# Places of the first small products behind the large ones, in a hybrid recurrent decoder step

## The chip, the cores and the metric

One core of a Trainium2 chip runs the whole step. The metric is the time of one execution on the device in microseconds, as a median over runs. TensorE (PE in the rows) multiplies, VectorE (DVE), ScalarE (ACT) and GpSimd (POOL) do the rest, SyncE (SP) issues the DMAs.

## What is computed

Two layers act on 1024 prompt tokens and 8 single tokens of width 1024. Cut to what matters here, a layer is:

```
h = rmsnorm(x, norm_g)
p = h @ w_in                       # split into q, f, i, z, ... of three groups
o_a = head_rmsnorm(gated_recurrence(q_a, k_a, i_a, log_f)) * silu(z_a)    # 6 heads, 64 x 64
o_b = head_rmsnorm(gated_recurrence(q_b, k_b, v_b, log_g)) * silu(z_b)    # 6 heads, 32 x 64
o_c = s5 group with its own gate
x + concat(o_a, o_b, o_c) @ w_out
```

The recurrence runs by chunks: within a chunk `att = k^T q` under a causal mask times v, and between chunks the carried state S times q. `head_rmsnorm` needs the mean square over each head's 64 rows, which is a product with a block of ones. The 8 single tokens each take one step of the same recurrences from given states.

## The kernel before, in words

**Large products.** A tile of 128 output columns of `w_in` or `w_out` is one `gemm_tile` (L302): three blocks of tokens (384, 384, 264), in each block 8 steps k, in each step three matmuls (high and low parts of weights and input). So a tile has 72 large products, written `ps_g` in the rows; only tile 0 of layer 0 writes to other banks, so that up to any time of layer 0 there have been 72 more than the rows of `ps_g` count. A layer has 25 tiles from `w_in`, in the order UC 2, VB 3, QB, KB, QK, VA 3, then F and Q in turn three times, ZB 3, ZC 2, ZA 3, and then 8 from `w_out`. Weights come by DMA and are split into `wh` (ACT) and `wl` (POOL and DVE in turn).

**Small work by threads.** Everything else is in Python generators. `tick()` lets each living thread go on to its next `yield`; `gemm_tile` ticks after the fourth step k of each block and after each block, thus after every 12 large products. The place of a small product in the program is so the number of large ones that stand before it. There are threads for the S5 group (`s5_thread`, then `glu`), for turning values (`turn`, transposes of `vf`), for the single tokens (`decode`, L918), for the two parts of the B group (`unit_b`, two and one pairs of heads; L1116) and the three pairs of A heads (`unit_a`, L968). A lock lets one of b0, b1, a0, a1, a2 into its products at a time. A tensor of one row per channel and one column per token takes one of 16 slots; `room(n)` (L106) ticks without any large product until n are free.

**A unit's steps.** `unit_a`: transposes of k, `kv()` (state updates, then scaled by DVE L1045 and scanned, L897), `att()`, two yields, `inter()` (state times q, rows `ps_o<-qs,Sp`), the masks of `att` (DVE, L1077), a yield, `intra()` (`ps_o<-atts,v`), then for each of two halves `headnorm` (L900) and a yield. `headnorm` squares and splits on ACT and DVE (`sl` L907), yields, multiplies with the ones (`ps_aux<-sl,obd`), then takes the root. `unit_b` has four (b0) or two (b1) rounds of a yield, `outputs` (L1184, rows `ps_o<-qb,Sp`), the next round's `att` and mask (L1181), and a `headnorm`. `decode` ends with one small product per token (`ps_aux<-dS,qbd`), a copy, a transpose (`ident,dV`), a copy and 4 or 8 small DMAs.

**The order of the work.** The launch says `schedule_with_timeline_sim=True`. A planner writes out each engine's order when the program is built, by a model of time of its own: among the instructions of an engine that it holds ready, the one that the program issued first goes next. On the chip each engine then keeps to that order. A dependency of class `NoSync` is an order for the planner alone; it makes no semaphore.

PSUM has three `g` banks for the large products, two `o` banks and three `aux` banks for the small ones.

Of the kernel before, what the change touches and what calls it, by code (L numbers as in the profile page):

```python
# [14 lines left out]
P = 128  # L15
# [23 lines left out]
def tile_hybrid_step(ctx: ExitStack, tc: tile.TileContext, a: dict, nl=NL, limit=RANGE):  # L39
# [42 lines left out]
    def psum(tag, shape=(P, 512), dt=F32):  # L82
        n = {"g": 3, "o": 2, "aux": 3}[tag]
        return ps.tile(list(shape), dt, tag=tag, bufs=n, name=nm("ps_" + tag))
# [60 lines left out]
    def act(out, in_, func, **kw):  # L145
        return S.activation(out=out, in_=in_, func=func, **kw)  # L146
# [8 lines left out]
    def mm(out, lhsT, rhs, start=True, stop=True):  # L155
        return TE.matmul(out=out, lhsT=lhsT, rhs=rhs, start=start, stop=stop)  # L156

    def behind(i, others):

        for x in others:  # L160
            tc.add_manual_dep(getattr(i, "ins", i), getattr(x, "ins", x).name,
                              mybir.DependencyInfo(mybir.DependencyClass.Sync, mybir.DependencyReason.DATA), reason="bank")


    ident = cst.tile([P, P], F32, name="ident")
    maskA = cst.tile([P, 64], I8, name="maskA")
# [135 lines left out]
    def gemm_tile(i, blocks, rhs, evac, last=True, ks=range(KD), banks="ggg"):  # L302

        for b in blocks:
            o, n = BLK[b]
            p = psum(banks[b]) if isinstance(banks[b], str) else banks[b]
            for j, k in enumerate(ks):
                wh, wl = W.get(i, k)
                rh, rl = rhs(k, b)
                mm(p[:, :n], wh, rh, start=(j == 0), stop=False)  # L310
                mm(p[:, :n], wh, rl, start=False, stop=False)
                mm(p[:, :n], wl, rh, start=False, stop=(j == KD - 1))
                if j == 3:
                    tick()
                if b == blocks[-1] and last:
                    W.do_split(4 * (i + 1) + min(3, (j + 1) // 2))
            evac(b, p[:, :n])
            if b == blocks[0]:
                W.do_split(4 * (i + 1) + 1)
            tick()  # L320
# [339 lines left out]
    def layer(l, slow=False):  # L660
# [239 lines left out]
        def headnorm(po, dst, n=512):  # L900

            sq = tmp("sq", [P, 512])
            sh = tmp("sh", [P, 512], F32R)
            sl = tmp("sl", [P, 512], F32R)
            act(out=sq, in_=po, func=AF.Square)
            act(out=sh, in_=sq, func=AF.Copy)
            V.tensor_tensor(out=sl, in0=sq, in1=sh.bitcast(F32), op=ALU.subtract)  # L907
            yield
            pn = psum("aux")
            mm(pn, obd, sl, start=True, stop=False)  # L910
            mm(pn, obd, sh, start=False, stop=True)
            rs = tmp("sq", [P, 512])
            act(out=rs, in_=pn, func=AF.Ln, scale=1.0 / 64.0, bias=epsc)
            act(out=rs, in_=rs, func=AF.Exp, scale=-0.5)
            run = lambda x: x.rearrange("p (c t) -> p c t", t=n)
            V.tensor_tensor(out=dst if n < 512 else run(dst), in0=run(po), in1=run(rs), op=ALU.mult)

        def decode(pr, nh, kd, f8, k8, q8, head0, u0, sin, sout):  # L918

            yield from dec_lock.take()  # L920
            qbd = tmp("qbd", [P, 8, 32])[:pr]
            G.memset(qbd, 0.0)
            for h in range(nh):
                V.tensor_copy(out=qbd[h * kd:(h + 1) * kd, :, h], in_=q8[h * kd:(h + 1) * kd, :])
            sbs = []
            for b0 in (0, 4):
                sb = tmp("dS", [P, 4, 64], bufs=2)[:pr]
                vb = tmp("dV", [P, 4, 64])[:pr]
                SY.dma_start(out=sb, in_=sin[:, b0:b0 + 4, :])
                for h in range(nh):  # L930
                    SY.dma_start(out=vb[h * kd:(h + 1) * kd], in_=vdd[b0:b0 + 4, (head0 + h) * 64:(head0 + h) * 64 + 64]
                                 .unsqueeze(0).to_broadcast([kd, 4, 64]))
                yield
                G.tensor_tensor(out=sb, in0=sb, in1=f8[:, b0:b0 + 4].unsqueeze(2).to_broadcast([pr, 4, 64]), op=ALU.mult)
                G.tensor_tensor(out=vb, in0=vb, in1=k8[:, b0:b0 + 4].unsqueeze(2).to_broadcast([pr, 4, 64]), op=ALU.mult)
                G.tensor_tensor(out=sb, in0=sb, in1=vb, op=ALU.add)
                yield
                SY.dma_start(out=sout[:, b0:b0 + 4, :], in_=sb)
                sbs.append(sb)
            yield  # L940

            po = psum("aux")
            for i, sb in enumerate(sbs):
                for b in range(4):
                    mm(po[32 * b:32 * b + 32, 64 * i:64 * i + 64], qbd[:, 4 * i + b, :], sb[:, b, :])
            stg = tmp("dV", [P, 4, 64]).rearrange("p a b -> p (a b)")[:, :P]
            act(out=stg, in_=po[:, :P], func=AF.Copy)
            po = psum("aux")
            TE.transpose(out=po[:, :P], in_=stg, identity=ident)
            stg = tmp("dO", [P, 4, 4])[:, :nh]  # L950
            act(out=stg, in_=po[:, :P].rearrange("p (b h) -> p h b", h=32)[:, :nh], func=AF.Copy)
            for h in range(nh):
                u, hf = divmod(h, 2)
                for i in range(2):
                    SY.dma_start(out=odec[64 * hf:64 * hf + 64, u0 + u, 4 * i:4 * i + 4], in_=stg[64 * i:64 * i + 64, h, :])
            dec_lock.give()
            decodes[0] += 1
# [10 lines left out]
        def unit_a(j, s1, s2, qs):  # L968
# [67 lines left out]
            def kv():  # L1036
                p = [psum("aux").rearrange("p (c v) -> p c v", v=64) for _ in range(2)]
                for c in range(16):
                    pr_, par = divmod(c, 2)
                    for h in range(2):  # L1040
                        mm(p[par][64 * h:64 * h + 64, pr_, :], ktm[64 * par:64 * par + 64, pr_, 64 * h:64 * h + 64],
                           vA[64 * par:64 * par + 64, pr_, (2 * j + h) * 64:(2 * j + h) * 64 + 64])
                x = on[:, :T].rearrange("p (v k r) -> p r k v", k=8, r=2)
                for par in range(2):
                    V.tensor_tensor(out=x[:, par], in0=p[par], in1=ac.rearrange("p (k r) -> p r k", r=2)[:, par]  # L1045
                                    .unsqueeze(2).to_broadcast([P, 8, 64]), op=ALU.mult)
                states(Sp, on, 16)
# [4 lines left out]
            def att():  # L1052
                p = [psum("aux") for _ in range(2)]
                for pair in range(8):
                    for par in range(2):
                        t0 = (2 * pair + par) * 64
                        for h in range(2):
                            mm(p[h][64 * par:64 * par + 64, pair * 64:pair * 64 + 64], kt[64 * h:64 * h + 64, t0:t0 + 64],
                               qt[64 * h:64 * h + 64, t0:t0 + 64])
                return p  # L1060

            def inter(po):

                for pair in range(8):
                    for par in range(2):
                        c = 2 * pair + par
                        for h in range(2):
                            ph = slice(64 * h, 64 * h + 64)
                            if c:
                                x = mm(po[par][ph, pair * 64:pair * 64 + 64], S3[ph, c - 1, :], qt[ph, c * 64:c * 64 + 64],  # L1070
                                       start=(pair == 1 - par), stop=False)
                                if pair == 7:
                                    yield x

# [16 lines left out]
            if j == 0:  # L1091
                for x in atts:
                    G.memset(x, 0.0)
            kv()
            p = att()
            yield
            yield
# [18 lines left out]
        def unit_b(ti, s, q, k):  # L1116
# [67 lines left out]
            def outputs(hp, hf, po):  # L1184

                for cc in range(4):
                    c = 4 * hf + cc
                    for g in range(2):
                        hd = 2 * hp + g
                        if c:  # L1190
                            mm(po[64 * g:64 * g + 64, cc * P:cc * P + P], S3[32 * hd:32 * hd + 32, c - 1, :],
                               q[32 * hd:32 * hd + 32, c * P:c * P + P], start=(cc == 1 - hf), stop=False)
                for cc in range(4):
                    for g in range(2):
                        hd = 2 * hp + g
                        mm(po[64 * g:64 * g + 64, cc * P:cc * P + P],
                           vB[:, 4 * hf + cc, (h0 + hd) * 64:(h0 + hd) * 64 + 64], db[g][:, cc, :],
                           start=False, stop=(cc == 3))
# [433 lines left out]
```

## Time and profile before

| what | us |
|---|---|
| median of 3 runs (1051.87 to 1053.72) | 1052.39 |
| the profiled execution | 1056.13 |
| its span, first to last instruction | 1054.2 |
| PE busy in it | 994.6 |

The profile is of one execution, 3.7 us longer than the median. Times in the rows are microseconds from the span's start. PE matmuls overlap and their ends are modelled, so that PE's time is better read from starts and from waits; "idle before" is time in which an engine stood still, with what released it.

### The profile page before, as it was taken

The page shows a single profiled execution, that of the slowest core. Times are in us where ns is not written, and L with a number is a line of the kernel's source. Part 1 is how long each engine was busy: PE and PEld are TensorE (multiplying, and loading weights), DVE is VectorE, ACT ScalarE, POOL GpSimd, SP SyncE. Part 2 cuts the span into 40 slices and gives each one's busy share as a digit, 9 for nine tenths or more (in the row PEclk, how much of TensorE's full clock was granted, in tenths as well). Part 3 has the DMA queues.
Part 4 walks back from the last instruction along what each step waited for, and adds up shares of the span by engine and source line. Part 5 has one row for each costly group of instructions (what it writes and reads, how often), then busy time and mean ns, then how long its engine had stood idle before and what let it go on. Part 6 is the DMA issues. An engine that isn't in the chain of part 4 may idle for free.

```text
span 1054.2 us, 20947 instructions
## 1 busy us (share of the span) xinstructions
PE 994.6 (94%) x8071; PEld 940.2 (89%) x8071; DVE 649.4 (62%) x1333; ACT 479.2 (45%) x995; POOL 472.2 (45%) x668
## 2 busy tenths in 40 slices
PE   6899999999999899999999999999999989999992
PEld 5788898899988799999999999888998988999991
DVE  8986745744767746685464682684388775553344
ACT  7334224554434656633332423445554475664431
POOL 4685754115355535542181476431344453552233
PEclk9999999899999989999999999999999998999996
DMA  7131131111111121144323114112111112112313
GB/s 245 46 107 51 42 107 46 59 50 56 54 40 38 57 73 60 48 137 136 128 78 92 48 41 113 45 47 61 41 56 53 41 53 70 54 48 88 116 51 135
DMA packets 78811, 76.77 MB, mean 73 GB/s; under 512 B 24524, under 2 KB 60652, under 8 KB 78700
## 3 DMA queue, kind: packets, MB, share of 16 engines
q1 hardware_dynamic: 78700, 75.33, 23.6%
q8 instruction: 65, 1.06, 0.4%
q14 instruction: 46, 0.38, 0.1%
HBM read 58.01 MB, written 15.53 MB: 70 GB/s over the span
## 4 chain that ended last, share of the span: by engine, by line
PE 68%; DVE 15%; POOL 7%; ACT 3%; issue 3%; DMA 2%; SPq 1%; DVEq 0%; POOLq 0%; ACTq 0%
PE ps_g L156 54%; PE ps_aux L156 8%; PE ps_o L156 5%; DVE s5W L584 1%; DVE Sp L897 1%; ACT ep L146 1%; DVE ep L873 1%; PE ps_aux L850 1%; POOL wl L289 1%; DVE onorm L1045 1%; DMA x<-in_xT 1%; ACT sg L146 1%; DVE wl L289 1%; DVE sl L907 1%; POOL s5E L364 1%
## 5 line engine op out<-in xcount | busy, mean ns | idle before, releaser
L156 PE MATMUL ps_g<-hh,wl 128*128 128x384 f32 (+1 forms) x1176 | 382.1, 326 | 4.5 <-POOL wl L289 4.5
L156 PE MATMUL ps_g<-hh,wh 128*128 128x384 f32 (+1 forms) x1176 | 384.6, 327 | 0.0
L156 PE MATMUL ps_g<-lo,wh 128*128 128x384 f32 (+1 forms) x1176 | 380.9, 324 | 0.0
L156 PEld LDWEIGHTS ps_g<-hh,wl 128*128 128x128 f32 x1176 | 223.5, 190 | 8.8 <-POOL wl L289 6.8
L156 PEld LDWEIGHTS ps_g<-hh,wh 128*128 128x128 f32 x1176 | 223.7, 190 | 5.3 <-issue 3.1
L156 PEld LDWEIGHTS ps_g<-lo,wh 128*128 128x128 f32 x1176 | 223.8, 190 | 1.0
L289 POOL TENSOR_TENSOR wl<-raw,wh 128x256 fp32r<-128x256 f32 x127 | 109.6, 865 | 219.9 <-ACT wh L146 207.0
L146 ACT ACTIVATE wh<-raw 128x256 fp32r<-128x256 f32 x258 | 102.2, 411 | 123.9 <-PE ps_g L156 111.5
L156 PE MATMUL ps_g<-m,wh 128*128 128x384 f32 (+1 forms) x567 | 135.7, 321 | 0.0
L289 DVE TENSOR_TENSOR wl<-raw,wh 128x256 fp32r<-128x256 f32 x131 | 82.1, 627 | 42.3 <-ACT wh L146 34.5
L156 PEld LDWEIGHTS ps_g<-m,wh 128*128 128x128 f32 x567 | 98.9, 188 | 0.5
L156 PE MATMUL ps_g<-m,wl 128*128 128x384 f32 (+1 forms) x261 | 82.9, 320 | 0.0
L1350 POOL TENSOR_TENSOR z<-z,sg 128x384 f32<-128x384 f32 (+1 forms) x48 | 47.3, 986 | 44.8 <-ACT sg L146 43.6
L156 PEld LDWEIGHTS ps_g<-m,wl 128*128 128x128 f32 x261 | 49.0, 188 | 0.1
L741 DVE TENSOR_TENSOR z<-ps_g,rn 128x384 f32<-128x384 f32 (+1 forms) x48 | 24.4, 509 | 32.8 <-PE ps_g L156 32.7
L146 ACT ACTIVATE sg<-z 128x384 f32<-128x384 f32 (+1 forms) x48 | 23.4, 487 | 28.9 <-DVE z L1348 28.7
L1360 DVE SCALAR_TENSOR_TENSOR onorm<-z,vec,onorm 128x384 f32<-128x384 f32 (+1 forms) x36 | 23.0, 639 | 21.3 <-POOL z L1350 21.2
L156 PE MATMUL ps_g<-vx,wh 128*128 128x384 f32 (+1 forms) x129 | 34.1, 322 | 0.0
L146 ACT ACTIVATE sg<-sg,ones 128x384 f32<-128x384 f32 (+2 forms) x52 | 32.3, 622 | 0.8
L146 ACT ACTIVATE sg<-sg 128x384 f32<-128x384 f32 (+2 forms) x56 | 31.8, 568 | 1.7 <-DVE sg L778 0.8
L156 PE MATMUL ps_o<-qs,Sp 64*64 64x64 f32 x360 | 23.4, 301 | 8.6 <-DVE Sp L897 8.6
L156 PEld LDWEIGHTS ps_o<-qs,Sp 64*64 64x64 f32 x360 | 21.2, 199 | 10.8 <-DVE Sp L897 9.6
(385 smaller groups left out, 1802.1 us busy)
## 6 DMA issues: line engine op xcount, KB each, us to landing
raw<-in_wf SPq DMA_DIRECT2D x100, 256.0 KB
raw<-in_wo SPq DMA_DIRECT2D x32, 256.0 KB
x<-in_xT SPq DMA_DIRECT2D x16, 192.0 KB
ext<-in_xT SPq DMA_DIRECT2D x16, 192.0 KB
x1d<-ext SPq DMA_DIRECT2D x16, 192.0 KB
ext<-x1d SPq DMA_DIRECT2D x16, 192.0 KB
usd<-ucp SPq DMA_DIRECT2D x4, 512.0 KB
s5U<-usd SPq DMA_DIRECT2D x32, 64.0 KB
```

The source lines that it names most:

```text
L146: return S.activation(out=out, in_=in_, func=func, **kw)
L156: return TE.matmul(out=out, lhsT=lhsT, rhs=rhs, start=start, stop=stop)
L289: e.tensor_tensor(out=wl, in0=r, in1=wh.bitcast(F32), op=ALU.subtract)
L364: e.tensor_tensor(out=dr, in0=dr, in1=t, op=ALU.subtract)
L584: V.tensor_tensor_scan(out=W_[:, ri, q], data0=m8[:, q0 + q:q0 + q + 1].to_broadcast([P, P]), data1=W_[:, ri, q], initial=0.0, op0=ALU.mul ...
L741: V.tensor_tensor(out=dst[:, o:o + n], in0=p, in1=rn[:, o:o + n], op=ALU.mult)
L850: TE.transpose(out=p[:, c * P:(c + 1) * P], in_=f[:, t0:t0 + P], identity=ident)
L873: V.tensor_tensor_scan(out=g[:, cs], data0=zero[:pr].to_broadcast([pr, ch]) if plus is None else plus[:, cs], data1=x[:, cs], initial=0.0, ...
L897: V.tensor_tensor_scan(out=s[:, :64 * n], data0=s[:, :64 * n], data1=kv[:, :64 * n], initial=0.0, op0=ALU.mult, op1=ALU.add)
L907: V.tensor_tensor(out=sl, in0=sq, in1=sh.bitcast(F32), op=ALU.subtract)
L1350: G.tensor_tensor(out=z[:, c], in0=z[:, c], in1=sg[:, c], op=ALU.mult)
L1360: V.scalar_tensor_tensor(out=on[:, c], in0=z[:, c], scalar=g, in1=on[:, c], op0=ALU.mult, op1=ALU.mult)
```

## The change

`gemm_tile` remembers the third matmul of each step k, the last large product that the program has issued. `paced(i)` orders i behind that one (no semaphore). It is put on the first product of `headnorm`, of `att` and `inter` in `unit_a`, of `outputs` in `unit_b`, and on the first product and the transpose of `decode`: 34 instructions per layer. Yields are added: one in `headnorm`, one in `decode` before its transpose, two in `unit_a` between `kv()` and `att()`. Nothing is computed otherwise.

```diff
+    front = [None]
+    def paced(i):
+        if front[0] is not None:
+            tc.add_manual_dep(getattr(i, "ins", i), getattr(front[0], "ins", front[0]).name,
+                              mybir.DependencyInfo(mybir.DependencyClass.NoSync, mybir.DependencyReason.DATA), reason="pace")
+        return i
...
-                mm(p[:, :n], wl, rh, start=False, stop=(j == KD - 1))
+                front[0] = mm(p[:, :n], wl, rh, start=False, stop=(j == KD - 1))
...
             V.tensor_tensor(out=sl, in0=sq, in1=sh.bitcast(F32), op=ALU.subtract)
             yield
+            yield
             pn = psum("aux")
-            mm(pn, obd, sl, start=True, stop=False)
+            paced(mm(pn, obd, sl, start=True, stop=False))
...
-                    mm(po[32 * b:32 * b + 32, 64 * i:64 * i + 64], qbd[:, 4 * i + b, :], sb[:, b, :])
+                    x = mm(po[32 * b:32 * b + 32, 64 * i:64 * i + 64], qbd[:, 4 * i + b, :], sb[:, b, :])
+                    if i + b == 0:
+                        paced(x)
...
             act(out=stg, in_=po[:, :P], func=AF.Copy)
+            yield
             po = psum("aux")
-            TE.transpose(out=po[:, :P], in_=stg, identity=ident)
+            paced(TE.transpose(out=po[:, :P], in_=stg, identity=ident))
...
+                            if t0 + h == 0:
+                                paced(x)
...
+                                if c + h == 1:
+                                    paced(x)
...
             kv()
+            yield
+            yield
             p = att()
             yield
             yield
...
+                            if cc == 1 - hf and g == 0:
+                                paced(x)
```

The last three are in `att` and `inter` of `unit_a` and in `outputs` of `unit_b`, each on the first matmul.

## Rows read from the trace of the kernel before

**Rows 1.** The page: busy time, share of the span, instructions.

```profile
PE 994.6 (94%) x8071; PEld 940.2 (89%) x8071; DVE 649.4 (62%) x1333; ACT 479.2 (45%) x995; POOL 472.2 (45%) x668
```

**Rows 2.** Waits of PE over the span: in total, times, longest.

```profile
PE ps_o L156 <- DVE Sp L897: 8.6, 6, 2.3
...
PE ps_aux L156 <- DVE sl L907: 4.2, 4, 2.4
PE ps_aux L156 <- DVE onorm L1045: 3.8, 2, 2.1
PE ps_aux L850 <- DVE atts L1181: 3.1, 2, 1.9
...
PE ps_aux L949 <- ACT dV L146: 0.8, 1, 0.8
```

**Rows 3.** Stages: window, its length, busy time of each engine, PEclk, DMA share, GB/s.

```profile
144.00:246.00 102.00, 100.09 (x887) 88.91 (x886) 56.45 (x106) 47.13 (x86) 31.20 (x37) 0.97 0.20 56
...
275.00:382.00 107.00, 96.49 (x1225) 90.84 (x1224) 70.08 (x131) 49.77 (x103) 49.02 (x54) 0.92 0.16 48
...
652.00:755.00 103.00, 101.57 (x907) 90.90 (x906) 59.35 (x100) 49.03 (x87) 33.04 (x36) 1.00 0.19 55
...
784.00:898.00 114.00, 106.25 (x1291) 100.14 (x1290) 79.86 (x151) 62.28 (x127) 51.12 (x58) 0.94 0.19 57
```

**Rows 4.** Matmuls of ps_g alone, counted (x) up to the start of a small run.

```profile
0.00:279.19 279.19, 177.53 (x1007) 0.98 0.26 78
0.00:284.74 284.74, 179.21 (x1015) 0.98 0.26 78
0.00:304.10 304.10, 191.08 (x1087) 0.98 0.26 76
0.00:314.63 314.63, 200.92 (x1138) 0.97 0.25 76
0.00:367.42 367.42, 232.06 (x1321) 0.97 0.24 72
0.00:155.65 155.65, 98.50 (x540) 0.98 0.33 100
0.00:163.72 163.72, 101.65 (x557) 0.98 0.32 97
0.00:173.13 173.13, 106.40 (x586) 0.98 0.31 94
```

**Rows 5.** PE in order of time, layer 0, B units: start, us, what [idle before].

```profile
181.96 0.51 PE L156 MATMUL ps_o<-qb,Sp 32*64 32x128 f32 x4
184.38 0.66 PE L850 MATMUL ps_aux<-ident,vf 128*128 128x128 f32 x4 [1.91 <-DVE atts L1181]
...
190.55 0.67 PE L156 MATMUL ps_g<-hh,wh 128*128 128x384 f32 x1
```

**Rows 6.** DVE in order of time, the same stretch.

```profile
178.94 4.15 DVE L584 TENSOR_TENSOR_SCAN s5W<-sm,s5W 128x128 f32<-128x128 f32 x4
183.02 0.66 DVE L907 TENSOR_TENSOR sl<-sq,sh 128x512 fp32r<-128x512 f32 x1
...
184.22 0.71 DVE L1181 COPY_PREDICATED atts<-maskB,ps_aux 128x512 f32<-128x512 int8 x1
```

**Rows 7.** PE, the same run of products in layer 1.

```profile
690.72 0.66 PE L850 MATMUL ps_aux<-ident,vf 128*128 128x128 f32 x4 [1.21 <-DVE atts L1181]
...
694.56 0.42 PE L156 MATMUL ps_g<-hh,wh 128*128 128x384 f32 x1
```

**Rows 8.** PE, large products and a run of small ones beside each other.

```profile
212.86 0.42 PE L156 MATMUL ps_g<-lo,wh 128*128 128x384 f32 x1
213.11 0.33 PE L156 MATMUL ps_g<-hh,wl 128*128 128x384 f32 x1
213.38 0.99 PE L156 MATMUL ps_o<-qk,Sp 32*64 32x128 f32 x12
...
217.79 0.33 PE L156 MATMUL ps_g<-lo,wh 128*128 128x384 f32 x1
217.96 0.34 PE L156 MATMUL ps_g<-hh,wl 128*128 128x384 f32 x1
```

**Rows 9.** The stretch after the wait of rows 5, columns as in rows 3.

```profile
185.10:191.90 6.80, 6.80 (x39) 5.16 (x40) 6.80 (x24) 3.29 (x8) 0.81 (x2) 0.50 0.01 2
```

More of the change, by code (lines that the diff above doesn't have):

```diff
@@ L1057, in att @@
                         for h in range(2):
-                            mm(p[h][64 * par:64 * par + 64, pair * 64:pair * 64 + 64], kt[64 * h:64 * h + 64, t0:t0 + 64],
-                               qt[64 * h:64 * h + 64, t0:t0 + 64])
+                            x = mm(p[h][64 * par:64 * par + 64, pair * 64:pair * 64 + 64],
+                                   kt[64 * h:64 * h + 64, t0:t0 + 64], qt[64 * h:64 * h + 64, t0:t0 + 64])
+                            if t0 + h == 0:
+                                paced(x)
                 return p
@@ L1190, in outputs @@
                         if c:
-                            mm(po[64 * g:64 * g + 64, cc * P:cc * P + P], S3[32 * hd:32 * hd + 32, c - 1, :],
-                               q[32 * hd:32 * hd + 32, c * P:c * P + P], start=(cc == 1 - hf), stop=False)
+                            x = mm(po[64 * g:64 * g + 64, cc * P:cc * P + P], S3[32 * hd:32 * hd + 32, c - 1, :],
+                                   q[32 * hd:32 * hd + 32, c * P:c * P + P], start=(cc == 1 - hf), stop=False)
+                            if cc == 1 - hf and g == 0:
+                                paced(x)
                 for cc in range(4):
```

## The prediction, made before the changed kernel was run

> **What bounds the kernel now.** I read the page first: PE is busy for 994.6 of 1054.2 us, no other engine for over 62% [rows 1], and PE works in order, so time is lost where PE stands still or runs at the low clock. The waits of PE come next [rows 2]. Those that the edit names are the first product of `inter` behind the state scan (8.6 us in six waits, one in each A unit of each layer), the head norm behind `sl` (4.2 us in four), the second half of `att` behind the evacuation of `kv` (3.8 us in two) and the single tokens' transpose (0.8 us): 17.4 us. Another 3.1 us are transposes of v (L850) that wait for an `aux` bank which a mask frees. The stages show where this lies [rows 3]: the A units (275 to 382 and 784 to 898 us) have a granted clock of 0.92 and 0.94, the B units 0.97 in layer 0 and 1.00 in layer 1. So waits and low clock sit together, mostly in the A units.
>
> **Do the new places reach these waits?** This decides the forecast. `paced` can only hold a small product back to its place in the program, and a yield moves that place by 12 large products. Both do nothing for a product that the planner already runs later than its place. So I count places by the code and compare with the trace [rows 4], adding the 72 of tile 0.
>
> A0 of layer 0 starts behind 13 tiles (936 large products) and reaches `kv` after 7 ticks: place 936 + 84 = 1020. The trace runs it behind 1007 + 72 = 1079, so 59 late. `inter` has place 1044 now and 1068 with the two new yields; the trace runs it behind 1015 + 72 = 1087. The first head norm has place 1068 now and 1104 then; the trace has 1159. The second has 1092 and 1140; the trace has 1210. The narrowest case I found is `inter` of A2: place 1332, new place 1380 (its lock is free two ticks later, and the two yields), trace 1321 + 72 = 1393. Even there 13 large products remain. So in the A units the planner already runs every one of these runs later than the new place, because by its own clock their inputs are ready late; PE then waits because VectorE is later still on the chip. Neither edge nor yield moves them, and the waits behind `Sp`, `sl`, `onorm` and `dV` should stay.
>
> In the B units it is otherwise. The first `outputs` of b0 has place 504 + 108 = 612 and runs behind 540 + 72 = 612: the place binds. Its first head norm has place 624, the trace 629, the new place 636; the second has 648, 658 and 672. So B's steps do move: by 7 to 14 large products at each head norm, and each next round by a further tick.
>
> **Part by part.** Nothing is added to or taken from any engine's work; the 34 ordered instructions of a layer get no semaphore, so nothing new queues behind a wait.
>
> *A units.* Moved in the program are two masks (DVE), `intra`, the squares, splits and roots of two head norms (ACT, DVE), a state copy (POOL) and one DMA on SP, past the weight splits on POOL and DVE and at most four half-tile weight loads on SP. Their priority against large-product work stays, since they run later than the new place. Against the next unit's start (exponentials on ACT, scans on DVE) the second head norm loses its precedence. That can shift a wait of PE either way; the bounds are the four `sl` waits, gone or once more: -4.2 to +4.2 us. I take 0, as the next unit's products are late too.
>
> *Single tokens.* The transpose, ACT's copy and 4 or 8 small DMAs on SP come a tick later. The results are used behind tile 17 at the earliest, 7 tiles after B's last decode by place, and tiles cover them: 0. Were that cover gone, one wait like today's 0.8 us would come.
>
> *B units, the gain.* In layer 0 PE stands 1.91 us before the v transposes [rows 5]: the last round's masks hold two `aux` banks, and they stand on DVE behind four S5 scans (4.15 us) and a head norm's split [rows 6]. Layer 1 shows the same run with 1.21 us [rows 7]. S5's thread gets no yields, while this last round's `att` comes two head norms, so 24 large products, later, about 4 us at 0.17 us each [rows 8]. Its place is then behind that of the transposes (both stand at the same tick now), which so take the bank first. I count both waits as gone: -3.1 us. The clock was at its low level (0.50, 1.2 of 2.4 GHz) for 6.8 us after the first of them [rows 9]. The same run from the transposes to the next large product takes 190.55 - 184.38 = 6.17 us in layer 0 and 694.56 - 690.72 = 3.84 us in layer 1 at full clock [rows 5, 7]; with the wait gone the difference goes: -2.3 us. The bounds are 0 (other waits take their place) and -5.4.
>
> *B units, the price.* b0 and b1 have six head norms, so b1 ends six ticks later. Counting slots by the code, three are free for F0 at tile 11 now; with b1's two inputs held longer they come only when S5's `glu` gives up its own, four ticks later. `room(3)` then ticks four times with no large product between, in either layer: b1's last round and `glu`'s last products follow each other directly. F0's 72 large products are ready to fill in, which speaks for a price of 0. They only come in where the planner, by its own clock, sees the small ones late. No row shows this, so I bound it: below by 0, and not below nothing, as it only takes cover away; above by one longest `sl` wait, 2.4 us [rows 2], and the 2.3 us of low clock behind it, 4.7 us per layer. I take one mean `sl` wait per layer, 4.2 / 4 = 1.05 us, as `sl` products are what stands there: +2.1 us.
>
> **The sum** is -3.1 - 2.3 + 2.1 = -3.3 us on the profiled 1056.13, so 1052.8. That execution was 3.7 us above the median, so for the median 1052.39 - 3.3 = 1049.1 us. With the bounds of the parts, this case reaches from about 1043 (-5.4 and -4.2) to 1052 us.
>
> **Rivals.**
> *The edges do hold in the A units.* If there the planner's clock runs ahead of what I counted by over 13 large products, the places bind and the 17.4 us of waits go with the B units' -3.3. It costs switches: a large product follows another after 0.17 us, a small run of 32 or 64 rows after 0.27 [rows 8], and two more gaps in six units make 12 x 0.10 = 1.2 us. That gives 1052.4 - 19.5 = about 1033, less if clock comes back too (0.08 x 107 and 0.06 x 114 us at most [rows 3]). Against it speak the counts above. Chance 0.10. The Trainium skill speaks against such splitting: TensorEngine Tiling, section Key Properties, says that changing the tiling mode drains TensorE. The trace agrees in direction, with 0.27 against 0.17 us; by that rule this rival would gain a little less.
>
> *Nothing that can be measured.* The masks of another B round meet the S5 scans, or the v transposes wait elsewhere, and what is won in one place is paid in another: 1052 us, within 2. For it speaks that 17.4 of the waits aren't touched. Chance 0.27.
>
> *Slower, by the ticks without cover.* At tile 11 of each layer b1's last round and `glu` need `aux` banks that only DVE frees, and PE stands before them. At the upper price, 2 x 4.7 = 9.4 us, and with the gain of 5.4 still there, it is 1052.4 + 4.0 = 1056.4. It decides from 2.7 us of waits per layer there. Against it: large products fill in wherever the planner sees the gap. Chance 0.16.
>
> **How the numbers follow.** My case has 0.47, the others 0.10, 0.27 and 0.16. A measurement of this kernel tells about 0.2%, 2.1 us, from no change. Of my 0.47, 0.38 lie beyond 2.1 us on the fast side, 0.06 within and 0.03 above; of the second rival's 0.27, 0.02, 0.23 and 0.02. So faster 0.38 + 0.10 + 0.02 = 0.50, same 0.06 + 0.23 = 0.29, slower 0.03 + 0.02 + 0.16 = 0.21. The range leaves out the first rival below (0.10) and what goes past the third above (about 0.08): 1041 to 1056.5. My own case alone has 1043 to 1052.
>
> **What would show it.** Right: `inter`, `att` and head norms of the A units stand behind the same counts of large products to within a few, and `Sp` still costs about 8.6 us in six waits; in the B units the head norms stand at places 636 and 672; the two waits on L1181 before v's transposes are gone and 185 to 192 us runs at full clock; between tiles 11 and 12 small products stand together. Wrong: `Sp` waits well under 8 us in all, or A's runs moved by a tick or more (then places do bind, the first rival); new waits of PE over 2.7 us per layer around tile 11 (the third); or the same waits on L1181 at another round (the second).

## The result and the profile after

The change made the kernel **slower**: 1069.37 us median against 1053.06 us, ratio 1.0155 with a 95% interval of 1.0137 to 1.0174. That is 16.3 us, and above the predicted range. The profiled executions stand closer together, 1067.95 against 1056.13 us (spans 1066.1 and 1054.2), because the one of before lay 3.1 us above its median and the one of after 1.4 us below. So the traces account for 11.8 of the 16.3 us.

TensorE on the page of after [rows 1]:

```profile
PE 998.2 (94%) x8071; PEld 942.0 (88%) x8071; DVE 652.2 (61%) x1333; ACT 493.8 (46%) x1005; POOL 468.0 (44%) x668
```

PE has the same work, 3.6 us more of it by the clock. Its waits after, the costliest first [rows 2]:

```profile
PE ps_o L156 <- DVE atts L1094: 12.4, 7, 3.6
PE ps_o L156 <- DVE Sp L906: 9.0, 5, 3.8
...
PE ps_aux L156 <- DVE sl L916: 4.2, 3, 2.8
PE ps_g L156 <- POOL wl L298: 3.8, 5, 1.3
PE ps_aux L859 <- DVE atts L1200: 2.8, 2, 1.7
...
PE ps_aux L156 <- DVE atts L1200: 1.3, 1, 1.3
```

The lines of the code moved by 9 to 19: `Sp` L897 is L906 now, `sl` L907 is L916, the masks of A L1077 are L1094, those of B L1181 are L1200. `Sp` and `sl` wait as before. The waits for `onorm` (3.8 us) and `dV` (0.8 us) are gone. The waits before the v transposes are still there (2.8 for 3.1 us), at an earlier round. And there is a new one, 12.4 us: `intra` waits for the A masks, which cost nothing before.

To see where the time went I cut both spans where equally many large products have begun. Lengths can then be compared directly, as each piece holds the same large products. The pieces end behind 576, 864, 1440, 2880, 3312 and 3888 rows of `ps_g`: B units of layer 0, A units of layer 0, (a piece without them, 258.3 and 258.9 us), B units and A units of layer 1, the end. Columns: stretch, length, busy time of PE, PEld, DVE, ACT and POOL, granted clock, DMA. Before:

```profile
171.26:255.70 84.44, 82.53 (x636) 74.93 (x635) 45.53 (x91) 42.49 (x72) 27.80 (x31) 0.96 0.18 52
255.70:394.90 139.20, 128.69 (x1424) 122.86 (x1423) 93.89 (x181) 69.67 (x139) 66.77 (x72) 0.94 0.18 54
...
653.20:771.50 118.30, 116.87 (x1005) 106.25 (x1004) 67.32 (x117) 56.15 (x99) 37.40 (x42) 1.00 0.18 52
771.50:906.00 134.50, 126.57 (x1423) 120.25 (x1422) 96.61 (x185) 74.26 (x150) 60.20 (x69) 0.95 0.19 56
906.00:1054.20 148.20, 128.37 (x807) 126.79 (x805) 66.93 (x123) 63.57 (x144) 53.31 (x58) 0.94 0.27 85
```

After:

```profile
171.20:256.40 85.20, 83.49 (x636) 74.97 (x635) 48.17 (x87) 47.95 (x76) 25.73 (x30) 0.98 0.17 48
256.40:396.00 139.60, 126.20 (x1421) 120.79 (x1420) 93.42 (x181) 68.70 (x137) 65.49 (x72) 0.95 0.18 54
...
654.90:777.40 122.50, 118.97 (x1005) 106.97 (x1004) 66.94 (x117) 62.97 (x104) 37.14 (x42) 1.00 0.17 50
777.40:920.60 143.20, 129.62 (x1423) 123.41 (x1422) 97.97 (x185) 75.12 (x150) 57.97 (x69) 0.93 0.17 53
920.60:1066.10 145.50, 127.98 (x807) 126.45 (x805) 66.64 (x123) 63.61 (x144) 53.29 (x58) 0.95 0.27 87
```

How well such a length repeats can be read from two of the runs below, `edges_only` (the edges without the yields) and `hn_a_only` (the head norms' yield in the A units alone): in their traces every engine has its instructions in the order of before (but for two of VectorE that start within 2 ns of each other). The same four pieces in `hn_a_only`:

```profile
168.58:252.85 84.27, 82.51 (x637) 75.03 (x635) 45.26 (x90) 42.49 (x72) 27.86 (x31) 0.96 0.18 52
252.85:391.95 139.10, 129.03 (x1424) 123.24 (x1422) 92.92 (x181) 69.59 (x138) 67.09 (x72) 0.94 0.19 54
...
650.61:768.86 118.25, 116.86 (x1006) 106.25 (x1005) 67.31 (x117) 56.10 (x99) 37.48 (x42) 1.00 0.18 52
768.86:903.51 134.65, 126.25 (x1423) 119.91 (x1422) 97.52 (x185) 74.25 (x150) 59.10 (x69) 0.96 0.20 56
```

In both runs the four lie within 0.5 us of those of before. Only the stretch ahead of them differs by more (168.6 and 168.9 us for 171.3).

Layer 1 pays: 4.2 us in the B units and 8.7 in the A units; the last piece takes 2.7 us less. In these A units PE stands 13.6 us instead of 7.9 (length less busy); its waits are 13.4 us instead of 8.0, and those on the masks, new, are 6.2 of them. The low clock takes 143.2 x 0.07 = 10.0 us instead of 134.5 x 0.05 = 6.7 (an estimate, here and below: length times the share of the clock that is missing). In the B units there is no low clock on either side; 2.1 us are more standing and 2.1 more work by the clock. Layer 0 looks even, but before has 84.44 x 0.04 = 3.4 us of low clock there and after half of that: at full clock its B units are some 2.5 us longer too.

Now the counts of large products (x) up to the start of small runs in after [rows 4]: the first two B head norms, `inter` of A0, and A0's two head norms.

```profile
0.00:165.21 165.21, 102.89 (x564) 91.19 (x564) 12.49 (x24) 0.98 0.32 96
0.00:178.90 178.90, 109.51 (x600) 96.86 (x600) 12.92 (x25) 0.98 0.31 94
0.00:286.25 286.25, 182.75 (x1028) 165.67 (x1028) 22.05 (x43) 0.98 0.26 79
0.00:309.60 309.60, 195.60 (x1100) 177.56 (x1100) 23.14 (x45) 0.98 0.25 75
0.00:318.57 318.57, 203.58 (x1152) 185.52 (x1152) 24.33 (x48) 0.98 0.25 75
```

With the 72 of tile 0, B's head norms stand at 636 and 672, as predicted. A's runs were to stay and did not: `inter` went from 1015 to 1028, the head norms from 1087 and 1138 to 1100 and 1152, each by over a tick (12). `att`'s first half, which stood right behind `kv` at 1007, now stands with `inter` at 1028.

Why `intra` waits is on VectorE. Its order around A0's masks in layer 0, before and after:

```profile
288.93 1.37 DVE L1077 COPY_PREDICATED atts<-maskA,ps_aux 128x512 f32<-128x512 int8 x2 [2.98 <-PE ps_o L156]
...
292.63 1.46 DVE L873 TENSOR_TENSOR_SCAN ep<-zero,s 128x64 f32<-128x64 f32 x3
```

```profile
285.73 1.04 DVE L989 TENSOR_SCALAR qs<-qs 128x1032 f32<-128x1032 f32 x1
290.19 0.17 DVE L995 TENSOR_TENSOR q<-qs,ep 128x8 f32<-128x8 f32 x1 [3.42 <-ACT ep L146]
290.46 0.35 DVE L934 COPY qbd<-q 64x8 f32<-64x8 f32 x2
295.26 1.33 DVE L882 TENSOR_TENSOR_SCAN ep<-zero,s 128x64 f32<-128x64 f32 x1 [4.45 <-POOL qs L997]
296.51 1.29 DVE L1094 COPY_PREDICATED atts<-maskA,ps_aux 128x512 f32<-128x512 int8 x2
```

Before, the masks run ahead of the next unit's decay scans. After, the first of these scans stands ahead of them, and it waits 4.45 us for GpSimd: the masks run 7.6 us later, while `inter` began only 1.5 us later (284.74 and 286.25).

### The profile page after: what moved, and what is told of

Read it like the earlier page. It is cut to its first block, busy times and chain, and to the rows that moved or that the text cites. A ratio compares the mean times of both kernels' runs of the same rounds, so it can differ in the third digit from the quotient of the medians.

```text
span 1066.1 us, 20972 instructions
## 1 busy us (share of the span) xinstructions
PE 998.2 (94%) x8071; PEld 942.0 (88%) x8071; DVE 652.2 (61%) x1333; ACT 493.8 (46%) x1005; POOL 468.0 (44%) x668
## 4 chain that ended last, share of the span: by engine, by line
PE 65%; DVE 17%; POOL 6%; ACT 4%; DMA 3%; issue 3%; SPq 1%; POOLq 0%; DVEq 0%; ACTq 0%
PE ps_g L156 51%; PE ps_aux L156 7%; PE ps_o L156 5%; DVE ep L882 2%; DVE sl L916 1%; DVE Sp L906 1%; DVE onorm L1058 1%; ACT ep L146 1%; PE ps_aux L859 1%; DMA x<-in_xT 1%; DMA raw<-in_wf 1%; POOL s5E L373 1%; POOL s5Bm L375 1%; POOL wl L298 1%; ACT sg L146 1%
## 5 line engine op out<-in xcount | busy, mean ns | idle before, releaser
L298 DVE TENSOR_TENSOR wl<-raw,wh 128x256 fp32r<-128x256 f32 x131 | 79.0, 603 | 41.2 <-ACT wh L146 33.4
L156 PE MATMUL ps_o<-atts,v 64*64 64x64 f32 (+1 forms) x576 | 25.1, 261 | 12.5 <-DVE atts L1094 12.4
L916 DVE TENSOR_TENSOR sl<-sq,sh 128x512 fp32r<-128x512 f32 x24 | 27.6, 1150 | 12.7 <-ACT sh L146 12.5
L156 PEld LDWEIGHTS ps_o<-atts,v 64*64 64x64 f32 (+1 forms) x576 | 19.3, 152 | 17.1 <-DVE atts L1094 14.1
```

The lines of the kernel that those rows point to most:

```text
L298: e.tensor_tensor(out=wl, in0=r, in1=wh.bitcast(F32), op=ALU.subtract)
```

## The experiments

All ratios are against the kernel before on the same chip. "B units" and "A units" are the pieces above. In the names of the runs att, hn and dec are the yields between `kv` and `att`, of the head norms and of the single tokens' `decode`, a and b the units; "out" names what is left out of the change.

### The edges alone

The changed kernel without its yields, in all three places like this one:

```diff
             yield
-            yield
             pn = psum("aux")
             paced(mm(pn, obd, sl, start=True, stop=False))
```

> The kernel before with the edges alone and none of the four yields. Theory (the edges never hold a product up, the yields alone move the time): 1053 us, ratio 1.000 within 0.002, and the same rows of waits as before (Sp 8.6 us, sl 4.2, onorm 3.8). Rival (the edges cost the time): 1060 us or more.

Measured: 1053.4 us, ratio 0.9996 (0.9979 to 1.0012). On every engine its instructions stand in the order of the kernel before. By themselves the edges do nothing, so that the loss comes with the yields. Of the runs below only `att_yields_out` and `after_masks_first` have the edges; none has all the yields without them, so that they do nothing there too is not shown.

### One yield at a time

Against the kernel before:

```diff
             kv()
+            yield
+            yield
             p = att()
```

> The kernel before with the two yields between kv and att alone. Theory (these two put att and with it the masks behind the single tokens' products and the next unit's scans; the 12.4 us of waits of the products of atts and v are theirs): 1063 to 1067 us, ratio 1.009 to 1.013, and the wait on the masks of 10 us or more is there. Rival (the loss comes from the yields of head norms and of the single tokens, in B and at tile 11): 1052 to 1055 us, no such wait.

Measured: 1049.57 us, ratio 0.9966 (0.9953 to 0.9979). The theory fell. The wait on the masks came (14.4 us), and yet the kernel is faster. Its waits of PE:

```profile
PE ps_o L156 <- DVE atts L1092: 14.4, 5, 6.8
...
PE ps_o L156 <- DVE Sp L906: 2.9, 3, 1.4
...
PE ps_g L156 <- POOL wl L298: 2.4, 5, 1.1
...
PE ps_aux L156 <- DVE sl L916: 1.0, 3, 0.5
```

The wait for `wl` was before:

```profile
PE ps_g L156 <- POOL wl L289: 4.5, 6, 1.3
```

Against before, `Sp` loses 5.7 us, `sl` 3.2, `onorm` 3.8 and `wl` 2.1, together 14.8 for 14.4: waits were swapped. The two profiled spans differ by 11.3 us, much more than the medians (4.2 us), and not all of it is the yields' doing: up to `att` of A0, some 274 us into the span, every engine has the order of before, and yet 2.3 us were saved ahead of the B units of layer 0 and 3.9 in them (80.59 us at full clock for 84.44 at 0.96). No moved work explains that; the low clock does, which came in one execution and not in the other. (`att_hn_a`, a run below with the same order up to there, has 82.8 us at 0.98. With the low clock taken off, all five executions of that order agree in this piece, at 80.6 to 81.2 us.) Behind `att`, the gain shows in the A units of layer 1, 129.65 us for 134.50:

```profile
765.63:895.28 129.65, 124.05 (x1424) 119.27 (x1422) 95.43 (x184) 72.89 (x147) 59.21 (x68) 0.97 0.20 58
```

The low clock takes 129.65 x 0.03 = 3.9 us there instead of 6.7. The changed kernel without these two yields, and the one with the head norms' yield only:

> The changed kernel without the two yields between kv and att (edges and the other two yields stay). Theory: 1051 to 1057 us, ratio 0.998 to 1.004, with no wait on the masks of the A units above 1 us. Rival (head norms and single tokens carry the loss): 1064 us or more.

Measured: 1058.2 us, ratio 1.006 (1.0037 to 1.0083), above the theory's range.

```diff
             V.tensor_tensor(out=sl, in0=sq, in1=sh.bitcast(F32), op=ALU.subtract)
             yield
+            yield
             pn = psum("aux")
```

> The kernel before with the one yield of the head norms alone. Theory: between 1050 and 1056 us: the waits of the B units' transposes on the masks only change their round, the waits on sl change by 1 to 2 us. Rival (the four times without large products behind tile 11 now pass more ticks): 1057 us or more, with waits of over 2.7 us in each layer around the last B units' head norms.

Measured: 1057.88 us, ratio 1.0042 (1.0029 to 1.0055). So part of the loss, 0.4%, comes with the head norms' yield alone. I parted it by units.

```diff
-        def headnorm(po, dst, n=512):
+        def headnorm(po, dst, n=512, lag=0):
...
             yield
+            yield from pause(lag)
             pn = psum("aux")
...
-                yield from headnorm(po, on[:, 512 * hf:512 * hf + 512])
+                yield from headnorm(po, on[:, 512 * hf:512 * hf + 512], 512, 1)
```

> The kernel before with the head norms' yield in the B units alone. Theory (what the head norms' yield costs by itself arises in the B units, where the trace of the run with all head norms has 4 us more in layer 0 and 6 more in layer 1 between two large products): 1058 to 1063 us. Rival (it is the A units'): 1053 us.

> The kernel before with the head norms' yield in the A units alone. Theory: 1050 to 1053 us, a gain of 0 to 3 us, since the A stretch of layer 0 was 2.7 us shorter in the run with all head norms. Rival (the yield costs in A also without the yields between kv and att): 1057 us or more.

(For A alone the 1 goes to the other call, `yield from headnorm(po[par], x[:, par], 64, 1)`.) Measured: **in B alone 1061.8 us, 1.0112** (1.0063 to 1.0160); in A alone 1053.05 us, 1.0000 (0.998 to 1.0019). The B units of the first, layer 0 and layer 1:

```profile
170.19:261.54 91.35, 88.74 (x636) 78.38 (x635) 48.85 (x87) 47.10 (x76) 25.15 (x31) 0.94 0.16 46
...
658.32:781.01 122.69, 120.73 (x1005) 107.88 (x1004) 68.46 (x117) 62.13 (x104) 36.71 (x42) 1.00 0.18 50
```

They are 6.9 and 4.4 us longer than before, more than the 7.7 us by which its span grew (1061.9 to 1054.2).

The traces show more about these runs. `hn_a_only` has the order of before on every engine: in the A units this yield alone moves nothing. And `hn_b_only` has the order of `hn_yield_only` on every engine (but for two instructions of VectorE that start within 2 ns of each other). So one order was measured twice, with 1.0042 (1.0029 to 1.0055) on one chip and 1.0112 (1.0063 to 1.0160) on another, where the medians lie 4.1 and 9.7 us above before. B's yield alone costs between 0.4 and 1.1%, and what makes the two differ is open. The same two pieces in `hn_yield_only`:

```profile
170.84:259.41 88.57, 87.09 (x636) 77.59 (x635) 49.18 (x87) 46.98 (x76) 25.52 (x31) 0.96 0.17 48
...
653.78:778.92 125.14, 123.55 (x1005) 109.89 (x1004) 68.77 (x117) 62.30 (x104) 36.86 (x42) 0.97 0.17 49
```

With the low clock taken off, the two executions are 4 to 5 us longer than before in layer 0 (85.9 and 85.0 for 81.1) and 3 to 4 in layer 1 (122.7 and 121.4 for 118.3).

### What the B units' yield does: tile 11

b0 has four head norms and keeps the lock of the core until the last, so b1 starts four ticks later: in hn_b_only its `kv` stands at 719 large products instead of 668 in layer 0 and at 3095 instead of 3042 in layer 1, in after at 700 and 3076. Its rounds then meet the gate's products (`yh`, `wg`) at the start of tile 11 (behind 720 and 3096), where by the code `room(3)` ticks and no large product is issued. In layer 1 the longest stretch around the start of tile 11 without a large product lasts 5.3 us before and 9.0 us after. Before and after, layer 1 (the last line is `ps_g` alone: only 0.08 us, the ends of two begun earlier):

```profile
724.62:729.89 5.27, 5.27 (x42) 3.79 (x41) 3.61 (x6) 3.88 (x7) 2.00 (x2) 1.00 0.02 4
```

```profile
728.85:737.86 9.01, 9.01 (x80) 7.14 (x79) 6.09 (x12) 3.91 (x7) 1.16 (x1) 1.00 0.19 62
728.85:737.86 9.01, 0.08 (x2) 0.01 (x1) 0.41 (x1) 1.00 0.19 62
```

Is it the late head norm, or the longer unit? One run keeps the lag and takes the tick out elsewhere; the other only adds a yield to each half.

```diff
-                yield
+                if i == 0:
+                    yield
                 po = psum("o")
                 outputs(hp, hf, po)
```

> The head norms' yield in the B units alone, with the yield ahead of the next half's outputs taken out, so that a half of a unit takes the ticks that it took before. Theory (what costs is the length of the unit, not the late head norm): 1050 to 1056 us, and the last B unit's kv at the same count of large products as before, within 15. Rival (the late head norms cost): 1058 us or more.

```diff
                 yield
+                if i:
+                    yield
                 po = psum("o")
...
+            yield
             core_lock.give()
```

> The kernel before with one more yield in each half of a B unit and the head norms at their old distance. Theory (the length of the unit costs: the last B unit begins some 50 large products later and its products fall among those of the gate and of the small recurrences): 1058 to 1064 us. Rival (the late head norms cost): 1051 to 1055 us.

Measured: with the old length 1060.6 us, 1.0064 (1.0041 to 1.0088); longer only 1062.69 us, 1.0102 (1.0063 to 1.0142). By the times neither won outright. The pieces tell more. Old length, B and A units of layer 1:

```profile
650.36:771.74 121.38, 120.24 (x1006) 107.57 (x1005) 69.22 (x117) 56.63 (x99) 38.53 (x42) 1.00 0.18 51
771.74:913.25 141.51, 129.66 (x1423) 123.11 (x1422) 96.26 (x185) 73.88 (x150) 59.68 (x69) 0.93 0.18 53
```

Longer only, the B units of layer 1:

```profile
657.72:787.71 129.99, 129.16 (x1006) 114.69 (x1004) 66.67 (x117) 63.38 (x104) 37.68 (x42) 0.92 0.17 47
```

Old length: b1's `kv` is at 679 (expected within 15 of 668), the B units cost 3.1 us more in layer 1 and 0.5 less in layer 0, and 7.0 us come up in the A units, whose small products stand within six large ones of where they stood before. Longer only: 11.7 us in the B units of layer 1. But the low clock is most of that: 129.99 x 0.08 = 10.4 us. With the low clock taken off on all sides, the old length costs 2.9 us in layer 0 (83.90 against 84.44 - 3.4) and 3.1 in layer 1, the longer unit 5.4 (88.20 x 0.98) and 1.3. So in the B units, at full clock and in one profiled execution each, the late head norm and the longer unit each cost some 6 to 7 us; neither theory explains it all, and the longer unit alone brings the long stretch in which the clock fell. Why the first run loses in A is open.

### Pairs

These put the edits above together, against the kernel before; the single tokens' yield is that of the change.

```diff
             act(out=stg, in_=po[:, :P], func=AF.Copy)
+            yield
             po = psum("aux")
```

> The two yields between kv and att and the head norms' yield in the A units, the rest as before. Theory (the loss of the whole is an interaction: behind the late masks one more tick before the head norms makes every next unit late, and the waits on Sp and on sl come back beside the one on the masks): 1058 to 1064 us, Sp waits of 8 us or more. Rival (it is the single tokens' yield, or the B units): 1049 to 1051 us as with the two yields alone, Sp waits of 3 us.

> The two yields between kv and att and the single tokens' yield, the rest as before. Theory (the single tokens' transpose one tick later changes little): 1049 to 1052 us. Rival (the single tokens' yield is what turns the gain of the two yields into a loss): 1056 us or more.

> The two yields between kv and att and the head norms' yield in the B units alone. If the two parts simply add: 0.9966 and 1.0112 give 1.008, 1060 us. Rival (they hinder each other, since the B units now end later and the A units start into them): 1066 us or more, with Sp waits of 8 us again.

> The two yields between kv and att and the head norms' yield in A and B, without the single tokens' yield. Theory (the single tokens' yield does nothing beside these): 1066 to 1071 us, as the whole change. Rival (it takes part in the loss): 1063 us or less.

| yields of | us | ratio | 95% |
|---|---|---|---|
| att + head norms of A | 1050.35 | 0.9986 | 0.9969 to 1.0004 |
| att + single tokens | 1049.35 | 0.9967 | 0.9947 to 0.9987 |
| att + head norms of B | 1059.16 | 1.0054 | 1.0031 to 1.0076 |
| att + head norms of A and B | 1063.89 | 1.0098 | 1.0068 to 1.0128 |
| all (the change) | 1069.37 | 1.0155 | 1.0137 to 1.0174 |

The interaction that I looked for between att and A's head norms is small (0.2%); Sp waits 4.8 us there, not 8. B's head norms cost about 0.9% on top of att (1.0054 / 0.9966), 1.1% with A's too. The parts of att and B together are near the sum (1.008 expected, 1.0054 found). The single tokens' yield does nothing beside att. The whole is 0.6% slower than the four yields without it, which came out between my theory and its rival; as that run also leaves out the edges, it is likely and not shown that this yield takes part in the loss. Where the two profiled executions part is the A units of layer 1: 134.8 us without the single tokens' yield, 143.2 with it.

The clock gives these runs another turn. In the B units of layer 1 the products of PE stand in the same order in hn_b_only and att_hn_b. The stretch of small products at tile 11, first in hn_b_only, then in att_hn_b:

```profile
732.29:743.13 10.84, 10.41 (x88) 8.17 (x87) 4.99 (x8) 5.50 (x7) 0.00 (x0) 1.00 0.08 27
```

```profile
723.41:739.78 16.37, 15.82 (x88) 11.88 (x87) 6.02 (x9) 7.20 (x9) 1.44 (x1) 0.61 0.06 18
...
727.00:744.00 17.00, 17.00 (x85) 13.81 (x86) 6.26 (x9) 4.77 (x6) 2.38 (x1) 0.50 0.00 1
```

The same 88 products, with at most 0.6 us of standing in each, once at full clock and once with 17 us at 0.50 (1.2 of 2.4 GHz), which lengthened the stretch by 5.5 us. With this stretch in the program the clock may fall in it: in layer 1 it did in five of the eight profiled executions with a b1 that begins over 30 large products later (`hn_yield_only`, `att_hn_b`, `att_hn`, `b_longer_only`, `after_masks_first`), and in the B units of layer 1 of one of the others, briefly. In layer 0, where the stretch lasts 9.2 to 10.4 us in these eight, it fell in none. `hn_yield_only` has the order of `hn_b_only`, so that the order doesn't decide it.

### VectorE's order in the A units

Three ways to take the masks' wait off, on att + single tokens: two more yields between `inter` and `intra`, two more ahead of the decay scans, or an order for the planner alone that puts each scan behind the last masks issued.

```diff
             yield
+            yield
+            yield
             intra(po)
```

> The run with the yields of att and of the single tokens, with two more yields between inter and intra. Theory (the 14.6 us of waits on the masks are true waits of TensorE; two ticks are 24 large products, some 4 to 6 us, longer than all but the 6.8 us wait): the waits on the masks fall to 4 us or less and the time to 1036 to 1045 us. Rival (what hangs on the masks moves on to the head norms and to the next unit, and the waits only change their names): 1048 to 1055 us.

```diff
             yield
+            yield
+            yield
             ep = epx[:, :T]
             ac, bm = yield from decay(ep, s1[:, :T], P, 64, 1.0, ep if l else None)
```

> The run with the yields of att and of the single tokens, with two more yields ahead of the decay scans of each A unit. Theory (the masks come late since the next unit's scans stand ahead of them on VectorE and wait for GpSimd): in layer 0 the masks now stand ahead of these scans, and the wait on the masks at about 288 us, 6.8 us long, goes; the time 1041 to 1047 us. Rival (the masks wait for inter's products, not for the scans): the 6.8 us stay, 1049 us or more.

```diff
                     behind(x, done)
+                    masked[:] = [x]
...
-                V.tensor_tensor_scan(out=g[:, cs], data0=zero[:pr].to_broadcast([pr, ch]) if plus is None else plus[:, cs],
+                y = V.tensor_tensor_scan(out=g[:, cs], data0=zero[:pr].to_broadcast([pr, ch]) if plus is None else plus[:, cs],
                                      data1=x[:, cs], initial=0.0, op0=ALU.add, op1=ALU.subtract)
+                for m in masked:
+                    tc.add_manual_dep(getattr(y, "ins", y), getattr(m, "ins", m).name,
+                                      mybir.DependencyInfo(mybir.DependencyClass.NoSync, mybir.DependencyReason.DATA), reason="order")
```

> The run with the yields of att and of the single tokens, with the masks of an A unit ahead of the next unit's decay scans on VectorE. Theory (VectorE's order makes the waits on the masks): the 14.6 us of waits on the masks fall to 5 us or less, 1037 to 1045 us. Rival (the masks come late for another reason, or the scans that now stand behind them make the next unit late): 1049 us or more.

Measured, first: 1052.84 us, 0.9999 (0.9985 to 1.0013). `intra` of A0 stands behind 1050 large products as without the two yields, and the masks' waits stay (15.8 us for 14.6): here the planner did run it later than its place. `Sp` waits 6.0 us for 3.5, and the gain of att + single tokens (0.9967) is gone, as the rival had it. Second: 1058.29 us, 1.0049 (1.0028 to 1.0069); the waits on the masks are gone, those on `Sp` (6.1 us for 3.5), `onorm` (3.1) and `wh` (3.9) came. Third: **1047.82 us, 0.9944** (0.9925 to 0.9963), the lowest of all, though its interval meets that of att + single tokens, and above the 1037 to 1045 us expected. Its waits:

```profile
PE ps_aux L156 <- DVE sl L920: 12.4, 3, 6.6
...
PE ps_o L156 <- DVE atts L1098: 2.1, 3, 1.6
```

The masks' 14.6 us fall to 2.1, so VectorE's order was what made them; but PE waits 12.4 us for `sl`, where it waited 0.9. In either order `sl` of A0 stands behind the scans; with the masks and `intra` early, it is what PE comes to next. The wait changed its name.

The same order in the changed kernel:

> The changed kernel with the masks of an A unit ahead of the next unit's decay scans on VectorE. Theory: the 12.4 us of waits on the masks fall to 5 us or less and the time by 5 to 10 us, to 1058 to 1064 us; the rest of the loss is the B units'. Rival: 1067 us or more, the waits on Sp and sl grow by what those on the masks lose.

Measured: 1064.24 us, 1.0094 (1.0061 to 1.0126), 0.6% below the whole change. Its A units of layer 1:

```profile
787.75:922.64 134.89, 125.14 (x1423) 119.54 (x1422) 96.57 (x184) 72.81 (x148) 59.37 (x69) 0.96 0.19 56
```

They take 134.9 us instead of the 143.2 of after: with the masks ahead, the largest piece of the loss is not there. (Its B units had the low clock at tile 11, so its span shows nothing of it.)

### The whole without B's head norms

Att, the single tokens and A's head norms, first as such and then with the masks ahead of the scans:

> The yields of the changed kernel without the one of the head norms in the B units (those between kv and att, of the A units' head norms and of the single tokens stay). Theory (the B units' yield is the loss, with all else in place too): ratio 0.997 to 1.001, 1049 to 1054 us. Rival (the yields of the A units and single tokens lose by themselves once they are together): 1060 us or more.

> The same with the masks of an A unit ahead of the next unit's decay scans. Theory (with masks ahead of the scans it is sl that comes late, 12.4 us of waits, and the A units' head norm yield gives it a tick of cover): the waits on sl fall to 6 us or less and the time is 1040 to 1046 us. Rival (the waits go on to the next unit's inter, which starts later too): 1048 to 1053 us.

Measured: without B's yield 1053.28 us, 1.002 (1.0001 to 1.0038); its A units of layer 1 take 133.02 us and there is again no stretch over 5.5 us without a large product around tile 11. So 1.0155 - 1.0020 = 1.35%, **14 of the 16 us**, hang on B's head norms (this run leaves out the edges, too). Such shares don't add up: without att's yields the change loses 0.95% less (1.0060), without the single tokens' 0.57% less (1.0098). The 8.7 us in the A units of layer 1 are gone in all three, with 133.0, 135.3 and 134.8 us for 143.2: it takes these yields together. With the masks first and A's head norms late too: 1052.54 us, 1.0014 (0.9991 to 1.0037); a miss, `sl` still waits 12.0 us.

## Why the prediction was wrong

*"Neither edge nor yields moves them": half right.* The edges bind nowhere in the kernel before, by the order and by the time (0.9996), and the first rival falls with them. Two more yields ahead of `intra` leave `intra` of A0 where it was, too. But the two ahead of `att` do move the A runs. They moved by 13 large products with no place that binds, so that my sign for the first rival, a move by a tick or more, came without it. I compared a run's place with large products alone. But `att` shares three `aux` banks with the single tokens' products and VectorE's queue with the next unit's scans; two ticks later in the program, it stands behind those (the first product of PE that differs in `att_yields_only` is a single tokens' one, ahead of `att` of A0). Alone this is worth -0.34%, 3.6 us, inside my bounds of 4.2 either way, with 14.8 us of waits swapped for 14.4. For the head norms of A the count was right: their yield alone leaves every engine's order as it was.

*B units, the gain: wrong.* Places 636 and 672 were right, the gain of 5.4 us was not there. The waits for masks in `aux` banks came at another round (2.8 us for 3.1, and 1.3 more before a head norm), as the second rival had it; of the 3.4 us that the low clock took in layer 0, half went.

*B units, the price: the step that failed.* I had the mechanism: the slots at tile 11, the ticks of `room(3)` without a large product, b1's last rounds and the gate's products next to each other. I priced it at 2.1 us, by one mean `sl` wait a layer, and bounded it at 4.7 us a layer by waits. But most of the price isn't a wait of PE: in the B units of layer 1 its waits grew by 2.1 us (3.5 for 1.4), under the 2.7 that were to tell. PE is busy, 9 us long in after, with nothing but small products, and the clock can fall in that stretch (10.4 us lost in `b_longer_only`); the late head norms cost by themselves as well. With price and gain my B units were to save 3.3 us; in the change they cost 0.8 and 4.2. B's yield alone costs 0.4 to 1.1%, 4 to 12 us, in the profile of `hn_b_only` 6.9 us in layer 0 (91.35 x 0.06 - 3.4 = 2.1 of it low clock) and 4.4 in layer 1. The third rival had place and sign; its price of 4.7 us was passed in layer 0 of that run alone, it kept a gain that never came, and it lacked the A units.

*A units: the other step that failed.* I took 0 for them, as the places don't bind there; in the traces 8.7 of the 11.9 us of the spans, the largest piece, lie in the A units of layer 1. They go when the masks are put ahead of the scans (134.9 us), when B's yield is taken out (133.0), which acts in units that end before this piece begins, and in the runs without att's (135.3) or the single tokens' yields (134.8). That the yields act together there is shown; by which step of the planner, is not.

*The range.* The parts' own upper bounds, 4.2 us for A and 9.4 for the price in B with no gain, add to 1066.0 us. My range stopped at 1056.5, as it took the upper price only with the gain and left A's bound out on that side.

*Single tokens: 0* held beside att (0.9967 and 0.9966), and probably not in the whole, where 0.6% more came with them and the edges.

## What to carry to other kernels

A step moved to a later place in the program is late on every queue that it uses, and holds its banks, slots and locks for longer: list what else stands on those, before asking what it hides behind. A thread made a few ticks longer was paid here at the next point where the large work stops, and the waits of the bounding engine showed only part of it; count the stretches without a large product. Compare each engine's order between runs before you read a difference in time: of mine, two repeated the kernel before and two each other, which tells how far a time or a piece repeats. And cut both spans at equal counts of a work that didn't change: this gave the stage that paid, where totals of waits only gave swaps.

## What the runs showed of the hardware

The low clock came while PE was busy without a break: 17.00 of 17.00 us at 0.50 in att_hn_b, begun about 1 us after a wait of 0.55 us and for its first 12.8 us (to 739.78) in small products only; the same products in hn_b_only had 1.00 throughout, and in hn_yield_only, with the same order as that on every engine, the clock fell. The Trainium skill (TensorE: Matmul & The Clock Gate, Part 1) puts the low level where the engine was idle. The rows show no such idleness here; as the ends of matmuls are modelled, short pauses between small products would not show in them. What decides between the runs stays open.

An order can also add work. ScalarE's table loads in the B units of layer 1, before and after:

```profile
L146 ACT ACT_TABLE_LOAD x1 | 1.3, 1283 | 0.7 <-PE ps_aux L156 0.7
```

```profile
L146 ACT ACT_TABLE_LOAD x6 | 7.7, 1283 | 2.1 <-DMA s5yk<-ydd 2.1
```

Five more of 1.28 us each: the roots of two late head norms now stand between the two halves of the S5 group's activation (`yc`), each root in two steps with a load before each, and one more load stands before the second half. All eight runs with the late b1 have 15 loads in their spans, the others 5. ScalarE has room (busy 62.97 of 122.50 us), but PE waited 1.1 us for `yh`, which stands on ScalarE behind the last of them, the second half of `yc` and one load more that before has as well (L153).
